# Signs turned and first-step weight sums moved to accumulating DMAs in the Strassen FFNs of a hybrid decoder step

## The chip, the core and the metric

The kernel runs on one core of a Trainium2 chip, in one launch. The metric is the device time of that launch in microseconds, the median of the runs shown. The engines are TensorE (PE, with its weight loads PEld), VectorE (DVE), ScalarE (ACT), GpSimd (POOL) and SyncE (SP, which issues nearly all DMAs).

## The reference

Two layers over 512 prompt rows and 32 sample rows, all fp32. Layer 0 has a gated MLP token mixer, layer 1 forgetting attention; both have two SwiGLU FFNs around the mixer and a gated per-layer embedding behind it:

```python
def swiglu(x, w1, w3, w2):
    return (jax.nn.silu(x @ w1) * (x @ w3)) @ w2
...
        for i in range(DEPTH):
            h = h + 0.5 * swiglu(rmsnorm(h, ffn1_norm[i]), ffn1_w1[i], ffn1_w3[i], ffn1_w2[i])
            xn = rmsnorm(h, mix_norm[i])
...
            h = h + mix
            h = h + 0.5 * swiglu(rmsnorm(h, ffn2_norm[i]), ffn2_w1[i], ffn2_w3[i], ffn2_w2[i])
            gate = jax.nn.sigmoid(rmsnorm(h, ple_norm[i]) @ ple_w_gate[i])
            h = h + gate * (pe[i] @ ple_w_proj[i])
```

D_MODEL is 1024, D_FF 2816, DEPTH 2: four FFNs in all. The change is in these four alone.

## The kernel before

Activations are kept transposed, 128 features by 544 rows (512 prompt, 32 sample), in eight tiles `h`. Every fp32 product is made of three float32r matmuls: an operand is split into a high part (a ScalarE copy with rounding) and the rest (a VectorE subtraction), and hi·hi, hi·lo, lo·hi are added in PSUM. For a weight block the split is `_split` (L190 the ScalarE cast, L191 the VectorE subtraction); `mm` (L233 to L239) does the matmuls.

All weights run through one stream of *pieces*, in the order in which TensorE uses them. `prepare` keeps the stream ahead of the piece in use: inside an FFN splits are made 2 pieces ahead, sums 3 and loads 6 (`self.ahead`). `_load` brings 512 KB by a DMA from SP into one of 44 buffers named `big`.

An FFN begins with four plain pieces (the first 256 columns of w1 and w3, of 48 matmuls each), whose results `gate` in `ffn` (L418 to L421) takes out of PSUM. Meanwhile `forms` (L299 to L306) makes the sums of halves of the activations. Then come ten Strassen steps, each on a 2x2 block of weights `a11, a12, a21, a22` (`seven`), with seven products in the order of `SEVEN = "1562734"` (`products`, L476, 24 matmuls each). Products 1, 2 and 4 use a block as it was loaded, the other four use sums of blocks, made on VectorE by `_sum` (L176), 128x1024 each:

```python
        for k, x, op, y in (("5", a21, "+", a22), ("6", (r, "5"), "-", a11), ("7", a11, "-", a21),
                            ("3", a12, "-", (r, "6"))):
            d[k] = dict(key=(r, k), sum=(x, op, y))
```

Products add into three PSUM tiles: A takes 1, 6, 7, 4, C takes 5, 3, B takes 2. After products 1, 5 and 6 ScalarE copies the tile out (`evict`, L484, to `r1`, `r5`, `r6`) before the next product goes on adding; so product 7, which adds to A, waits for the copy `r6`. From step 2 on, products of the second matrix (w2) stand between these.

Inside the steps (`ffn_steps`) the instruction order of PE, ACT, DVE and POOL is the written one; elsewhere the scheduler sets it. Every engine takes its instructions in order. POOL adds squares of the activations (L318) at an FFN's end, and has little else; no DMA is issued from it. The four FFNs are called FFN 1 to 4 in order of time.

Of the kernel before, what the change touches and what calls it, by code (L numbers as in the profile page):

```python
# [23 lines left out]
F32R = mybir.dt.float32r  # L24
I32 = mybir.dt.int32
AF = mybir.ActivationFunctionType
ALU = mybir.AluOpType
AX = mybir.AxisListType

P = 128  # L30
# [7 lines left out]
HT = T // 2  # L38
# [48 lines left out]
class Builder:  # L87
# [45 lines left out]
    def flat(self, n, dt=F32):  # L133
        return self.big(dt)[:].rearrange("p a b -> p (a b)")[:, :n]

    def add_plain(self, ap):
        r = len(self.aps)
        self.aps.append(ap)
        self.pieces.append(dict(key=(r, 0), src=(r, 0), n=ap.shape[1], sum=None))

    def seven(self, aps):

        r = len(self.aps)
        self.aps.extend(aps[k] for k in (0, 2, 3, 1))
        a11, a21, a22, a12 = ((r + k, 0) for k in range(4))
        d = {k: dict(key=(r, k), src=x, sum=None) for k, x in (("1", a11), ("2", a12), ("4", a22))}
        for k, x, op, y in (("5", a21, "+", a22), ("6", (r, "5"), "-", a11), ("7", a11, "-", a21),
                            ("3", a12, "-", (r, "6"))):
            d[k] = dict(key=(r, k), sum=(x, op, y))
        for v in d.values():  # L150
            v.update(n=1024)
        return d

    def _load(self):
        ap = self.aps[self.a_load]
        raw = self.flat(1024)
        self.nc.sync.dma_start(out=raw[:, :ap.shape[1]], in_=ap)
        self.raws[self.a_load] = raw
        self.a_load += 1

    def _raw(self, x, n):
        r, c = x
        while self.a_load <= r:
            self._load()
        return self.raws[r][:, c:c + n]

    def _sum(self):
        p = self.pieces[self.p_sum]
        self.p_sum += 1
        if p["sum"] is None:  # L170
            return
        a, op, b = p["sum"]
        get = lambda x: self._raw(x, 1024) if isinstance(x[1], int) else self.sums[x]
        a, b = get(a), get(b)
        t = self.flat(1024)
        self.nc.vector.tensor_tensor(t, a, b, ALU.add if op == "+" else ALU.subtract)  # L176
        self.sums[p["key"]] = t

    def _split(self):
        while self.p_sum <= self.p_split:  # L180
            self._sum()
        p = self.pieces[self.p_split]
        n = p["n"]
        src = self.sums[p["key"]] if p["sum"] else self._raw(p["src"], n)
        if n <= 512:
            w = self.flat(1024, F32R)
            hi, lo = w[:, :n], w[:, 512:512 + n]
        else:
            hi, lo = (self.flat(n, F32R) for _ in range(2))
        self.nc.scalar.copy(hi, src)  # L190
        self.nc.vector.tensor_tensor(lo, src, hi.bitcast(F32), ALU.subtract)  # L191
        self.split[self.p_split] = (hi, lo)
        self.p_split += 1

    def prepare(self):

        u, end = self.p_next, len(self.pieces) - 1
        split, sums, load = self.ahead
        while self.p_split <= min(u + split, end):
            self._split()  # L200
        while self.p_sum <= min(u + sums, end):
            self._sum()
        p = self.pieces[min(u + load, end)]
        need = [x for x in (p["sum"][::2] if p["sum"] else [p["src"]]) if isinstance(x[1], int)]
        while self.a_load <= max([r for r, _ in need], default=0):
            self._load()

# [86 lines left out]
    def forms(self, h, gcol, n, xs):  # L294

        nc = self.nc
        x = self.big()
        for a in range(2):
            nc.scalar.activation(x[:, a, :], h[2 * n + a], AF.Copy, scale=self.gain(gcol + 2 * n + a))  # L299
        t13, t24 = self.tmp(), self.tmp()  # L300
        two = lambda t: t.rearrange("p (a b) -> p a b", a=2)
        f13, f24 = self.big(F32R), self.big(F32R)
        nc.vector.tensor_tensor(two(t13), x[:, :, HT:], two(x[:, 0, :]), ALU.subtract)
        self.split_pair(f13, t13)
        nc.vector.tensor_tensor(t24[:, :HT], x[:, 1, HT:], t13[:, :HT], ALU.subtract)
        nc.vector.tensor_tensor(t24[:, HT:], x[:, 1, :HT], t24[:, :HT], ALU.subtract)  # L306
        self.split_pair(f24, t24)
        half = lambda t, b: tuple(x[:, b * HT:(b + 1) * HT] for x in t)
        f13, f24 = ((t[:, 0, :], t[:, 1, :]) for t in (f13, f24))
        return {"1": half(xs[2 * n], 0), "2": half(xs[2 * n + 1], 0), "3": half(xs[2 * n + 1], 1),  # L310
                "5": half(f13, 0), "7": half(f13, 1), "6": half(f24, 0), "4": half(f24, 1)}
    def ssq(self, acc, h, cols=slice(0, T), first=False):

        nc = self.nc
        sq = acc[:, cols] if first else self.tmp()[:, cols]
        nc.scalar.activation(sq, h[:, cols], AF.Square)  # L316
        if not first:
            nc.gpsimd.tensor_tensor(acc[:, cols], acc[:, cols], sq, ALU.add)  # L318
# [60 lines left out]
    def ffn_pieces(self, n):  # L379
        i, d = self.i, {}  # L380
        for f in range(2):
            for w in range(2):
                self.add_plain(i["w13p"][n, w, f])
        for kind, at, k, part in self.ffn_slots():
            if kind == "g":
                if at not in d:
                    d[at] = self.seven([i["w13"][n, at - 1, x] for x in range(4)])
                self.pieces.append(d[at][k])
            elif at < len(PARTS) - 1:
                if k % 2 == 0:  # L390
                    self.aps.append(i["w2a"][n, at, k // 2])
                    d["w"] = len(self.aps) - 1
                src = d["w"], k % 2 * 512
                self.pieces.append(dict(key=src, src=src, n=512, sum=None))
            elif part is None or part[0] == 0:
                self.add_plain(i["w2b"][n, k])
# [36 lines left out]
    def ffn_steps(self, h, xf, rstd, first, on_chunk):  # L433
        nc = self.nc
        add = ALU.add
        tt = nc.vector.tensor_tensor
# [4 lines left out]

        def gate(j, a, g):

            def one():
                tt(g, g, rstd.unsqueeze(1).broadcast_to([P, 2, T]), ALU.mult)  # L445

            def two():
                nc.scalar.activation(g[:, 0], g[:, 0], AF.Silu)  # L448

            def three():  # L450
                tt(g[:, 1], g[:, 1], g[:, 0], ALU.mult)

            def four():
                pair = self.big(F32R)
                self.split_pair(pair, g[:, 1])
                hid[j, a] = pair[:, 0, :], pair[:, 1, :]
            return [one, two, three, four]
# [22 lines left out]
        def evict(j, k):  # L480
            t = tiles[j]
            if k in "156":
                t["r" + k] = q2(self.tmp())
                nc.scalar.copy(t["r" + k], t["C" if k == "5" else "A"])  # L484
                return
            if k == "2":
                t["g"] = self.big(), self.big()
            g = t["g"]
            if k == "2":
                for w in range(2):  # L490
                    tt(g[0][:, w, :HT], t["B"][w], t["r1"][:, w], add)
            elif k == "7":
                tt(g[1][:, :, HT:], t["A"], t["r5"], add)
            elif k == "3":
                tt(g[0][:, :, HT:], t["C"], t["r6"], add)
                todo[0].extend(gate(j, 0, g[0]))
            else:
                nc.scalar.copy(g[1][:, :, :HT], t["A"])  # L498
                todo[1].extend(gate(j, 1, g[1]))
                del tiles[j]  # L500
# [858 lines left out]

# [22 lines left out]
```

## Time and profile before

| | |
|---|---|
| median of 3 runs | 2092.16 us (2091.04 to 2095.01) |
| profiled execution | 2090.37 us, of which the span is 2088.2 |
| PE busy | 2053.9 us, 98% of the span |
| DVE busy | 1521.5 us, 73% |
| ACT busy | 934.8 us, 45% |
| POOL busy | 181.0 us, 9% |
| DMA moved | 237.94 MB, mean 114 GB/s |

In the profile a line L176 is line 176 of the kernel. "issue" is time in which an engine waited for nothing that the profile shows. Starts are counted from the beginning of the span. Matmuls overlap, so the time shown of a group exceeds the distance between the starts of two groups.

### The profile page before, as it was taken

Reading aid. Unit: us, or ns where it says so; the run is one execution under the profiler, and the core shown is the slowest. Engines: PE = TensorE matmul, PEld = TensorE weight load, DVE = VectorE, ACT = ScalarE, POOL = GpSimd, SP = SyncE. Lnnn points to the kernel's source line nnn. Section 1 sums busy time; section 2 is a strip of 40 time slices with the busy share of each in tenths; the row PEclk is TensorE's granted clock in tenths of the full one; section 3 lists DMA queues with packets and bytes.
Section 4 is the critical chain, followed back from the end, with each engine's and each line's share of the span. In section 5 each row is a group of like instructions: output and inputs, shape, how many; then the busy total and the mean of one; then the engine's idle time right before and its main releaser. Section 6 shows DMA issues by size and latency. Waiting matters only on the chain.

```text
span 2088.2 us, 38796 instructions
## 1 busy us (share of the span) xinstructions
PE 2053.9 (98%) x16364; PEld 2016.3 (97%) x16364; DVE 1521.5 (73%) x1893; ACT 934.8 (45%) x1376; POOL 181.0 (9%) x226
## 2 busy tenths in 40 slices
PE   6999999999999999999999999999999999999999
PEld 6999999999999999999999999999977999999999
DVE  7877787556787777776698777786465887777773
ACT  6444344423445344454355344444364654343451
POOL 0000000410100000042050000001041300000020
PEclk9999999999999999999999999999999999999999
DMA  4232324312223232432193322326467322322331
GB/s 163 90 112 73 111 93 140 104 54 71 73 101 117 75 103 81 152 97 81 47 323 148 112 101 91 112 74 198 156 196 267 105 102 72 111 85 98 123 102 44
DMA packets 93776, 237.94 MB, mean 114 GB/s; under 512 B 9490, under 2 KB 27442, under 8 KB 93602
## 3 DMA queue, kind: packets, MB, share of 16 engines
q1 hardware_dynamic: 93458, 235.42, 33.8%
q8 instruction: 129, 2.11, 0.4%
q14 instruction: 45, 0.37, 0.1%
q10 hardware_dynamic: 144, 0.04, 0.0%
HBM read 218.94 MB, written 16.49 MB: 113 GB/s over the span
## 4 chain that ended last, share of the span: by engine, by line
PE 88%; DVE 5%; ACT 3%; DMA 2%; issue 1%; SPq 0%; POOL 0%; ACTq 0%; DVEq 0%; POOLq 0%
PE ps L476 33%; PE ps L233 14%; PE ps L239 14%; PE ps L237 14%; PE pb L476 5%; ACT big L190 1%; DVE big L191 1%; DVE big L176 1%; PE ps L1144 1%; PE ps L1146 1%; PE ps L1145 1%; PE ps L992 0%; PE ps L990 0%; PE ps L1105 0%; DMA big<-in_w13p 0%
## 5 line engine op out<-in xcount | busy, mean ns | idle before, releaser
L476 PE MATMUL ps<-big,big 128*128 128x272 f32 x5760 | 750.2, 289 | 10.6 <-DVE tmp L418 5.3
L476 PEld LDWEIGHTS ps<-big,big 128*128 128x128 f32 x5760 | 735.7, 189 | 12.4 <-ACT tmp L484 6.9
L191 DVE TENSOR_TENSOR big<-big,big 128x1024 fp32r<-128x1024 f32 (+2 forms) x541 | 594.6, 1101 | 107.9 <-ACT big L190 107.7
L190 ACT CAST big<-big 128x1024 fp32r<-128x1024 f32 (+2 forms) x541 | 489.4, 932 | 282.5 <-DVE big L176 275.3
L233 PE MATMUL ps<-big,big 128*128 128x256 f32 x2768 | 576.2, 289 | 12.0 <-ACT big L289 8.8
L239 PE MATMUL ps<-big,big 128*128 128x256 f32 x2768 | 570.9, 288 | 1.0 <-DVE big L191 1.0
L237 PE MATMUL ps<-big,big 128*128 128x256 f32 x2768 | 571.2, 287 | 0.1
L233 PEld LDWEIGHTS ps<-big,big 128*128 128x128 f32 x2768 | 443.5, 189 | 15.4 <-ACT big L289 8.8
L237 PEld LDWEIGHTS ps<-big,big 128*128 128x128 f32 x2768 | 445.9, 189 | 0.6 <-DVE big L290 0.6
L239 PEld LDWEIGHTS ps<-big,big 128*128 128x128 f32 x2768 | 442.8, 188 | 1.8 <-DVE big L191 1.2
L318 POOL TENSOR_TENSOR st<-st,tmp 128x544 f32<-128x544 f32 (+1 forms) x63 | 87.3, 1386 | 1610.9 <-ACT tmp L316 1610.6
L176 DVE TENSOR_TENSOR big<-big,big 128x1024 f32<-128x1024 f32 x160 | 194.9, 1218 | 0.0
L515 DVE SCALAR_TENSOR_TENSOR big<-ps,big 128x544 f32<-128x544 f32 x160 | 115.6, 722 | 106.9 <-PE ps L239 106.7
L484 ACT COPY tmp<-ps 128x544 f32<-128x544 f32 x120 | 73.5, 612 | 146.5 <-PE ps L476 146.2
L476 PE MATMUL pb<-big,big 128*128 128x272 f32 x960 | 127.1, 288 | 0.0
L448 ACT ACTIVATE big<-big 128x544 f32<-128x544 f32 x80 | 52.8, 661 | 161.8 <-DVE big L445 160.0
L476 PEld LDWEIGHTS pb<-big,big 128*128 128x128 f32 x960 | 123.2, 188 | 0.0
L445 DVE TENSOR_TENSOR big<-big,st 128x1088 f32<-128x1088 f32 x80 | 103.2, 1290 | 10.0 <-ACT big L498 8.5
L289 ACT ACTIVATE big<-big,gains 128x544 fp32r<-128x544 f32 (+1 forms) x80 | 55.9, 703 | 118.9 <-DVE big L515 64.9
L278 DVE TENSOR_TENSOR big<-big,big 128x544 fp32r<-128x544 f32 (+1 forms) x96 | 69.5, 724 | 29.0 <-ACT big L277 28.6
L290 DVE SCALAR_TENSOR_TENSOR big<-big,gains,big 128x544 fp32r<-128x544 f32 (+1 forms) x80 | 64.6, 810 | 21.8 <-ACT big L289 21.8
L277 ACT CAST big<-big 128x544 fp32r<-128x544 f32 (+1 forms) x96 | 61.9, 644 | 27.0 <-DVE big L769 15.2
(189 smaller groups left out, 1267.0 us busy)
## 6 DMA issues: line engine op xcount, KB each, us to landing
big<-in_w SPq DMA_DIRECT2D x160, 512.0 KB
big<-in_w2a SPq DMA_DIRECT2D x64, 512.0 KB
big<-in_w2b SPq DMA_DIRECT2D x32, 384.0 KB
big<-in_w13p SPq DMA_DIRECT2D x16, 512.0 KB
big<-in_win SPq DMA_DIRECT2D x16, 512.0 KB
big<-in_wg SPq DMA_DIRECT2D x16, 512.0 KB
big<-in_wkv SPq DMA_DIRECT2D x16, 512.0 KB
big<-in_ck SPq DMA_DIRECT2D x16, 512.0 KB
```

What stands on the lines that cost most here:

```text
L176: self.nc.vector.tensor_tensor(t, a, b, ALU.add if op == "+" else ALU.subtract)
L190: self.nc.scalar.copy(hi, src)
L191: self.nc.vector.tensor_tensor(lo, src, hi.bitcast(F32), ALU.subtract)
L233: i = nc.tensor.matmul(out[:, a:b], wh, xh[:, a:b], start=s, stop=False)
L237: nc.tensor.matmul(out[:, a:b], wh, xl[:, a:b], start=False, stop=False)
L239: nc.tensor.matmul(out[:, a:b], wl, xh[:, a:b], start=False, stop=e)
L278: self.nc.vector.tensor_tensor(pair[:, 1, cols], src, pair[:, 0, cols].bitcast(F32), ALU.subtract)
L318: nc.gpsimd.tensor_tensor(acc[:, cols], acc[:, cols], sq, ALU.add)
L445: tt(g, g, rstd.unsqueeze(1).broadcast_to([P, 2, T]), ALU.mult)
L476: nc.tensor.matmul(dst[w], a[:, c], b, start=k in "152" and kp == 0 and n == 0, stop=kp == NKP - 1 and n == 2, skip_group_check=True)
L484: nc.scalar.copy(t["r" + k], t["C" if k == "5" else "A"])
L515: nc.vector.scalar_tensor_tensor(h[c], whole(out), 0.5, h[c], ALU.mult, ALU.add)
```

## The change

In step 1 of each FFN the four sums are no longer made on VectorE. A block is loaded by SP as before, and further blocks are added onto the same buffer by DMAs that POOL issues with `accum_op=ALU.add` (`_more`). The five buffers are: `u` = a11, later + a21 for product 7; `t` = a21 + a22 for product 5; `v` = a21 + a22 + a11 for product 6, later + a12 for product 3; a12; and a22. "Later" means: issued behind the split that reads the buffer's first content (in `_split`), and so waiting for it. That is five accumulating DMAs of 512 KB per FFN, and 5 SP loads where there were 4. Steps 2 to 10 keep their sums on VectorE. Since a DMA can only add, the signs of all forms are turned: weight sums become additions in all steps, the activation forms are other differences, and one of the two gate results has the opposite sign, which `gate` sets right by a scale of Silu and a scalar factor. The parameter `dynamic_dma_scratch_size` goes from 1024 to 4096.

```diff
-    def seven(self, aps):
-
-        r = len(self.aps)
-        self.aps.extend(aps[k] for k in (0, 2, 3, 1))
-        a11, a21, a22, a12 = ((r + k, 0) for k in range(4))
-        d = {k: dict(key=(r, k), src=x, sum=None) for k, x in (("1", a11), ("2", a12), ("4", a22))}
-        for k, x, op, y in (("5", a21, "+", a22), ("6", (r, "5"), "-", a11), ("7", a11, "-", a21),
-                            ("3", a12, "-", (r, "6"))):
-            d[k] = dict(key=(r, k), sum=(x, op, y))
+    def seven(self, aps, dma):
+
+        a11, a12, a21, a22 = aps
+        if dma:
+            u, t, v = self.add_load(a11), self.add_load(a21, a22), self.add_load(a21, a22, a11)
+            b, d = self.add_load(a12), self.add_load(a22)
+            return {k: dict(key=(t, k), src=(r, 0), n=1024, sum=None, more=more) for k, r, more in (
+                ("1", u, a21), ("5", t, None), ("6", v, a12), ("2", b, None), ("7", u, None), ("3", v, None),
+                ("4", d, None))}
+        r = [self.add_load(x) for x in (a11, a21, a22, a12)]
+        x11, x21, x22, x12 = ((k, 0) for k in r)
+        d = {k: dict(key=(r[0], k), src=x, sum=None) for k, x in (("1", x11), ("2", x12), ("4", x22))}
+        for k, x, y in (("5", x21, x22), ("6", (r[0], "5"), x11), ("7", x11, x21), ("3", x12, (r[0], "6"))):
+            d[k] = dict(key=(r[0], k), sum=(x, y))
...
-        self.nc.sync.dma_start(out=raw[:, :ap.shape[1]], in_=ap)
+        self.nc.sync.dma_start(out=raw[:, :aps[0].shape[1]], in_=aps[0])
+        for ap in aps[1:]:
+            self._more(raw, ap)
...
+    def _more(self, raw, ap):
+        self.nc.gpsimd.dma_start(out=raw, in_=ap, accum_op=ALU.add)
...
-        self.nc.vector.tensor_tensor(t, a, b, ALU.add if op == "+" else ALU.subtract)
+        self.nc.vector.tensor_tensor(t, a, b, ALU.add)
...
         self.nc.vector.tensor_tensor(lo, src, hi.bitcast(F32), ALU.subtract)
+        if p.get("more") is not None:
+            self._more(src, p["more"])
...
-        nc.vector.tensor_tensor(t24[:, :HT], x[:, 1, HT:], t13[:, :HT], ALU.subtract)
-        nc.vector.tensor_tensor(t24[:, HT:], x[:, 1, :HT], t24[:, :HT], ALU.subtract)
...
+        minus = lambda out, a, b: nc.vector.scalar_tensor_tensor(out, a, -1.0, b, ALU.mult, ALU.subtract)
+        minus(t64[:, :HT], t57[:, :HT], x[:, 1, HT:])
+        minus(t64[:, HT:], t64[:, :HT], x[:, 1, :HT])
...
-                    d[at] = self.seven([i["w13"][n, at - 1, x] for x in range(4)])
+                    d[at] = self.seven([i["w13"][n, at - 1, x] for x in range(4)], at == 1)
...
-                nc.scalar.activation(g[:, 0], g[:, 0], AF.Silu)
+                nc.scalar.activation(g[:, 0], g[:, 0], AF.Silu, scale=sign)
...
-                tt(g[:, 1], g[:, 1], g[:, 0], ALU.mult)
+                nc.vector.scalar_tensor_tensor(g[:, 1], g[:, 1], sign, g[:, 0], ALU.mult, ALU.mult)
...
-    nc = _bacc.Bacc("TRN2", target_bir_lowering=False, num_devices=1, dynamic_dma_scratch_size=1024)
+    nc = _bacc.Bacc("TRN2", target_bir_lowering=False, num_devices=1, dynamic_dma_scratch_size=4096)
```

The order of instructions changes at three places that matter below. First VectorE at the start of FFN 1, from the split of product 5's weights to that of product 3's. Before (L191 splits, L176 sums, L303 to L306 and L278 the activation forms, L418 to L421 the gate of the plain pieces):

```order
L191 TENSOR_TENSOR big70_411<-big61_341,big69_410 128x1024
L176 TENSOR_TENSOR big71_414<-big61_341,big32_172 128x1024
L303 TENSOR_TENSOR tmp74_470<-big73_467 128x544
L305 TENSOR_TENSOR tmp75_471<-big73_467,tmp74_470 128x272
L418 TENSOR_TENSOR tmp78_481<-ps63_347,st38_227 128x544
L420 TENSOR_TENSOR tmp79_482<-ps72_418,st38_227 128x544
...
L191 TENSOR_TENSOR big83_518<-big71_414,big82_517 128x1024
L191 TENSOR_TENSOR big85_522<-big49_259,big84_521 128x1024
L176 TENSOR_TENSOR big86_525<-big32_172,big47_255 128x1024
L191 TENSOR_TENSOR big91_557<-big86_525,big90_556 128x1024
L176 TENSOR_TENSOR big92_560<-big49_259,big71_414 128x1024
L191 TENSOR_TENSOR big97_593<-big92_560,big96_592 128x1024
```

And of the change (L203 splits, L318 and L320 forms, L434 and L436 gate; `big33` is t, `big34` v, `big32` u):

```order
L203 TENSOR_TENSOR big69_413<-big33_174,big68_412 128x1024
L318 TENSOR_TENSOR tmp72_470<-big71_467 128x544
L320 SCALAR_TENSOR_TENSOR tmp73_471<-tmp72_470,big71_467 128x272
L434 TENSOR_TENSOR tmp76_481<-ps62_349,st40_234 128x544
L436 TENSOR_TENSOR tmp77_482<-ps70_418,st40_234 128x544
...
L203 TENSOR_TENSOR big81_518<-big34_177,big80_517 128x1024
L203 TENSOR_TENSOR big83_523<-big49_262,big82_522 128x1024
L203 TENSOR_TENSOR big89_558<-big32_172,big88_557 128x1024
L203 TENSOR_TENSOR big94_592<-big34_177,big93_591 128x1024
```

The sums are gone, one more of them ahead of what is shown; the rest keeps its order here. In FFN 2 the forms moreover go ahead of L436, behind which they stood.

Second ScalarE in the same stretch, in the change (L202 casts, L501 the copies r1, r5, r6; a wait on DMASW is one for an accumulating DMA):

```order
L202 CAST big80_517<-big34_177 128x1024 [waits DMASW2_49]
L202 CAST big82_522<-big49_262 128x1024 [waits DMAHW2_49]
L501 COPY tmp87_555<-ps79_492 128x544 [waits PE_49,Activation_49]
L202 CAST big88_557<-big32_172 128x1024 [waits DMASW3_49]
L501 COPY tmp92_589<-ps86_530 128x544 [waits PE_49,Activation_49]
L202 CAST big93_591<-big34_177 128x1024 [waits DMASW4_49]
L501 COPY tmp97_621<-ps79_492 128x544 [waits PE_49,Activation_49]
```

The order is that of before. The cast for product 3 (of `big34`) stands ahead of the copy r6 (to `tmp97`) and now waits for an accumulating DMA where it waited for a VectorE sum.

Third POOL ahead of FFN 3, in the change (`big1492` is t, `big1491` u, `big1493` v; L788 and L335 were there before, next to each other):

```order
L788 COPY ks_112<-big1366_11387 128x32 [waits DVE_49] x2
L173 DMA big1492_12238<-in_w13 128x1024 [waits DMAHW7_49,PE_49]
L173 DMA big1491_12236<-in_w13 128x1024 [waits DMAHW6_49,DVE_49]
L173 DMA big1493_12241<-in_w13 128x1024 [waits DMAHW0_49,DMASW4_49,PE_49]
L173 DMA big1493_12241<-in_w13 128x1024 [waits DMASW4_49]
L173 DMA big1493_12241<-in_w13 128x1024 [waits DMASW5_49,DVE_49]
L335 TENSOR_TENSOR st1946_15998<-st1946_15998,tmp1948_16018 128x544 [waits DMAHW3_49,DMAHW2_49,Activation_49]
```

All five DMA rows are new: one addition to t, one to u, three to v. In FFN 3 the addition to u, which waits for VectorE's split of product 1, stands ahead of all three to v; in FFN 1, 2 and 4 the first two to v stand ahead of it.

## Rows read from the trace of the kernel before

**Rows 1.** The page's first part: busy time, share of the span and instructions of the engines.
```profile
PE 2053.9 (98%) x16364; PEld 2016.3 (97%) x16364; DVE 1521.5 (73%) x1893; ACT 934.8 (45%) x1376; POOL 181.0 (9%) x226
```

**Rows 2.** Busy time by stretch: length, PE, PEld, DVE, ACT, POOL (instructions), granted PE clock, DMA share, GB/s. The body of FFN 1, the start of FFN 2, and two stretches behind gaps of PE (FFN 1, FFN 4).
```profile
64.00:360.00 296.00, 296.00 (x2367) 296.00 (x2366) 230.31 (x264) 128.44 (x177) 0.00 (x0) 1.00 0.31 104
573.80:587.00 13.20, 12.55 (x98) 12.11 (x96) 10.67 (x14) 7.77 (x11) 0.00 (x0) 1.00 0.46 159
46.20:51.20 5.00, 4.99 (x24) 4.81 (x24) 4.70 (x8) 4.11 (x6) 0.00 (x0) 0.60 0.30 122
1685.00:1688.00 3.00, 2.92 (x13) 2.92 (x14) 2.11 (x2) 0.89 (x2) 0.00 (x0) 0.52 0.28 115
```

**Rows 3.** Timeline of PE, L476, at the starts of the four FFNs: start, us, operation, count, idle before and its releaser. 24 matmuls are one product; step 1 begins with products 1, 5, 6, then 2 (on pb), then 7.
```profile
37.77 3.18 PE L476 MATMUL ps<-big,big 128*128 128x272 f32 x24
46.21 5.02 PE L476 MATMUL ps<-big,big 128*128 128x272 f32 x24 [5.26 <-DVE tmp L418]
58.65 18.31 PE L476 MATMUL ps<-big,big 128*128 128x272 f32 x144 [0.88 <-ACT tmp L484]
...
573.85 9.62 PE L476 MATMUL ps<-big,big 128*128 128x272 f32 x72
587.34 4.92 PE L476 MATMUL ps<-big,big 128*128 128x272 f32 x37 [0.84 <-ACT tmp L484]
...
1115.93 6.20 PE L476 MATMUL ps<-big,big 128*128 128x272 f32 x48
1129.71 5.55 PE L476 MATMUL ps<-big,big 128*128 128x272 f32 x42 [0.90 <-ACT tmp L484]
...
1676.80 6.29 PE L476 MATMUL ps<-big,big 128*128 128x272 f32 x48
1685.09 4.82 PE L476 MATMUL ps<-big,big 128*128 128x272 f32 x24 [2.00 <-ACT tmp L484]
1689.74 3.18 PE L476 MATMUL pb<-big,big 128*128 128x272 f32 x24
1692.76 7.44 PE L476 MATMUL ps<-big,big 128*128 128x272 f32 x58
```

**Rows 4.** Timeline of DVE at the start of FFN 1: the first three sums (L176), the gate's first step, and the splits of products 6 and 2 (L191 x2).
```profile
37.18 1.22 DVE L176 TENSOR_TENSOR big<-big,big 128x1024 f32<-128x1024 f32 x1
43.09 1.22 DVE L176 TENSOR_TENSOR big<-big,big 128x1024 f32<-128x1024 f32 x1
45.34 0.72 DVE L418 TENSOR_TENSOR tmp<-ps,st 128x544 f32<-128x544 f32 x1
49.97 2.36 DVE L191 TENSOR_TENSOR big<-big,big 128x1024 fp32r<-128x1024 f32 x2 [0.22 <-ACT big L190]
52.25 1.22 DVE L176 TENSOR_TENSOR big<-big,big 128x1024 f32<-128x1024 f32 x1
```

**Rows 5.** Timeline of ACT at the start of FFN 1: the casts of products 7 and 3 (L190), and the copy r6 (L484) behind the second.
```profile
53.50 1.05 ACT L190 CAST big<-big 128x1024 fp32r<-128x1024 f32 x1 [2.11 <-DVE big L176]
57.03 1.05 ACT L190 CAST big<-big 128x1024 fp32r<-128x1024 f32 x1 [1.97 <-DVE big L176]
57.99 0.60 ACT L484 COPY tmp<-ps 128x544 f32<-128x544 f32 x1
```

**Rows 6.** Timeline of DVE in FFN 2 to 4: in FFN 2 the gate's step that needs the last plain product, two form instructions (L306, L278) right behind it, and the splits of 6 and 2; in FFN 3 the split of product 1, and the splits of 6 and 2; the same two in FFN 4.
```profile
574.72 0.71 DVE L420 TENSOR_TENSOR tmp<-ps,st 128x544 f32<-128x544 f32 x1
575.35 0.43 DVE L306 TENSOR_TENSOR tmp<-big,tmp 128x272 f32<-128x272 f32 x1
575.70 0.71 DVE L278 TENSOR_TENSOR big<-tmp,big 128x544 fp32r<-128x544 f32 x1
...
578.72 2.36 DVE L191 TENSOR_TENSOR big<-big,big 128x1024 fp32r<-128x1024 f32 x2 [0.23 <-ACT big L190]
...
1107.34 1.22 DVE L191 TENSOR_TENSOR big<-big,big 128x1024 fp32r<-128x1024 f32 x1 [0.23 <-ACT big L190]
1121.03 2.36 DVE L191 TENSOR_TENSOR big<-big,big 128x1024 fp32r<-128x1024 f32 x2 [0.23 <-ACT big L190]
...
1683.61 2.36 DVE L191 TENSOR_TENSOR big<-big,big 128x1024 fp32r<-128x1024 f32 x2 [0.22 <-ACT big L190]
```

**Rows 7.** The chain that ended last: two pieces in which it followed a 512 KB load from its issue on SP to the release of its reader (start, us, what).
```profile
15.77 3.54 DMA big<-in_w13p
1062.88 7.01 DMA big<-in_wkv
```

**Rows 8.** Busy time by stretch (columns as in Rows 2), around one 512 KB load that SP issued alone at 561.74.
```profile
562.00:562.50 0.50, 0.50 (x6) 0.50 (x5) 0.46 (x1) 0.00 (x0) 0.00 (x0) 1.00 0.00 0
...
564.50:565.00 0.50, 0.50 (x6) 0.50 (x5) 0.17 (x1) 0.29 (x1) 0.00 (x0) 1.00 0.17 66
```

**Rows 9.** Groups by line of DVE: count, busy us, mean ns; the weight sums, the gate's product, and a SCALAR_TENSOR_TENSOR of the same shape elsewhere.
```profile
L176 DVE TENSOR_TENSOR big<-big,big 128x1024 f32<-128x1024 f32 x160 | 194.9, 1218 | 0.0
L451 DVE TENSOR_TENSOR big<-big 128x544 f32<-128x544 f32 x80 | 57.4, 717 | 0.0
L808 DVE SCALAR_TENSOR_TENSOR big<-big,tmp 128x544 f32<-128x544 f32 x6 | 4.3, 722 | 0.1
```

**Rows 10.** Timelines of SP and POOL: one issue of a 512 KB load, and one of POOL's additions of squares.
```profile
561.74 0.33 SPq L157 DMA_DIRECT2D big<-in_w  x1
551.74 1.37 POOL L318 TENSOR_TENSOR st<-st,tmp 128x544 f32<-128x544 f32 x1 [4.46 <-ACT tmp L316]
```

More of the change, by code (lines that the diff above doesn't have):

```diff
@@ L134, in flat, with add_load @@
         return self.big(dt)[:].rearrange("p a b -> p (a b)")[:, :n]
+    def add_load(self, *aps):
+        self.aps.append(aps)
+        return len(self.aps) - 1
     def add_plain(self, ap):
-        r = len(self.aps)
-        self.aps.append(ap)
+        r = self.add_load(ap)
         self.pieces.append(dict(key=(r, 0), src=(r, 0), n=ap.shape[1], sum=None))
-    def seven(self, aps):
-        r = len(self.aps)
-        self.aps.extend(aps[k] for k in (0, 2, 3, 1))
-        a11, a21, a22, a12 = ((r + k, 0) for k in range(4))
-        d = {k: dict(key=(r, k), src=x, sum=None) for k, x in (("1", a11), ("2", a12), ("4", a22))}
-        for k, x, op, y in (("5", a21, "+", a22), ("6", (r, "5"), "-", a11), ("7", a11, "-", a21),
-                            ("3", a12, "-", (r, "6"))):
-            d[k] = dict(key=(r, k), sum=(x, op, y))
+    def seven(self, aps, dma):
[11 more added lines that the diff above has]
+            d[k] = dict(key=(r[0], k), sum=(x, y))
         for v in d.values():
@@ L154, in _load @@
     def _load(self):
-        ap = self.aps[self.a_load]
+        aps = self.aps[self.a_load]
         raw = self.flat(1024)
-        self.nc.sync.dma_start(out=raw[:, :ap.shape[1]], in_=ap)
+        self.nc.sync.dma_start(out=raw[:, :aps[0].shape[1]], in_=aps[0])
+        for ap in aps[1:]:
+            self._more(raw, ap)
         self.raws[self.a_load] = raw
         self.a_load += 1
+    def _more(self, raw, ap):
+        self.nc.gpsimd.dma_start(out=raw, in_=ap, accum_op=ALU.add)
     def _raw(self, x, n):
@@ L171, in _sum @@
             return
-        a, op, b = p["sum"]
-        get = lambda x: self._raw(x, 1024) if isinstance(x[1], int) else self.sums[x]
-        a, b = get(a), get(b)
+        a, b = (self._raw(x, 1024) if isinstance(x[1], int) else self.sums[x] for x in p["sum"])
         t = self.flat(1024)
-        self.nc.vector.tensor_tensor(t, a, b, ALU.add if op == "+" else ALU.subtract)
+        self.nc.vector.tensor_tensor(t, a, b, ALU.add)
         self.sums[p["key"]] = t
@@ L203, in prepare @@
         p = self.pieces[min(u + load, end)]
-        need = [x for x in (p["sum"][::2] if p["sum"] else [p["src"]]) if isinstance(x[1], int)]
+        need = [x for x in (p["sum"] or [p["src"]]) if isinstance(x[1], int)]
         while self.a_load <= max([r for r, _ in need], default=0):
@@ L299, in forms @@
             nc.scalar.activation(x[:, a, :], h[2 * n + a], AF.Copy, scale=self.gain(gcol + 2 * n + a))
-        t13, t24 = self.tmp(), self.tmp()
+        t57, t64 = self.tmp(), self.tmp()
         two = lambda t: t.rearrange("p (a b) -> p a b", a=2)
-        f13, f24 = self.big(F32R), self.big(F32R)
-        nc.vector.tensor_tensor(two(t13), x[:, :, HT:], two(x[:, 0, :]), ALU.subtract)
-        self.split_pair(f13, t13)
-        nc.vector.tensor_tensor(t24[:, :HT], x[:, 1, HT:], t13[:, :HT], ALU.subtract)
-        nc.vector.tensor_tensor(t24[:, HT:], x[:, 1, :HT], t24[:, :HT], ALU.subtract)
-        self.split_pair(f24, t24)
+        f57, f64 = self.big(F32R), self.big(F32R)
+        q = x[:].rearrange("p a (c b) -> p (a c) b", c=2)
+        nc.vector.tensor_tensor(two(t57), q[:, 0::3, :], q[:, 1:2, :].broadcast_to([P, 2, HT]), ALU.subtract)
+        self.split_pair(f57, t57)
+        minus = lambda out, a, b: nc.vector.scalar_tensor_tensor(out, a, -1.0, b, ALU.mult, ALU.subtract)
+        minus(t64[:, :HT], t57[:, :HT], x[:, 1, HT:])
+        minus(t64[:, HT:], t64[:, :HT], x[:, 1, :HT])
+        self.split_pair(f64, t64)
         half = lambda t, b: tuple(x[:, b * HT:(b + 1) * HT] for x in t)
-        f13, f24 = ((t[:, 0, :], t[:, 1, :]) for t in (f13, f24))
+        f57, f64 = ((t[:, 0, :], t[:, 1, :]) for t in (f57, f64))
         return {"1": half(xs[2 * n], 0), "2": half(xs[2 * n + 1], 0), "3": half(xs[2 * n + 1], 1),
-                "5": half(f13, 0), "7": half(f13, 1), "6": half(f24, 0), "4": half(f24, 1)}
+                "5": half(f57, 0), "7": half(f57, 1), "6": half(f64, 0), "4": half(f64, 1)}
     def ssq(self, acc, h, cols=slice(0, T), first=False):
@@ L390, in ffn_pieces @@
                 if k % 2 == 0:
-                    self.aps.append(i["w2a"][n, at, k // 2])
-                    d["w"] = len(self.aps) - 1
+                    d["w"] = self.add_load(i["w2a"][n, at, k // 2])
                 src = d["w"], k % 2 * 512
@@ L442, in gate @@
         def gate(j, a, g):
+            sign = 1.0 - 2 * a
             def one():
```

## The prediction

> **What bounds the kernel now.** The page's first part comes first [rows 1]: TensorE is busy 98% of the span, VectorE 73%. That alone says that work taken off VectorE is worth nothing unless it stands where TensorE waits. So the next view is busy time by stretch [rows 2]: in the body of FFN 1 (64 to 360 us) TensorE is busy all 296 us at full clock. There is nothing to gain there; the sums of steps 2 to 10 are covered. What is left is the start of each FFN, and the timeline of TensorE [rows 3] shows it. One product takes 3.02 us (1689.74 to 1692.76). Product 7 is the fifth in order, so without a wait it starts 4 x 3.02 = 12.08 us behind product 1. It starts late by:
>
> - FFN 1: 58.65 - (37.77 + 12.08) = 8.80 us
> - FFN 2: 587.34 - 585.93 = 1.41
> - FFN 3: 1129.71 - 1128.01 = 1.70
> - FFN 4: 1692.76 - 1688.88 = 3.88
>
> That is 15.8 us, 0.76% of the time, and all that this change can reach. Part of it is clock: behind gaps of 5.26 and 2.00 us the granted clock is 0.60 and 0.52 (near 1.2 GHz instead of 2.4), and the next product takes 5.02 and 4.82 us, 1.8 to 2.0 too many; behind gaps of 0.84 us it stays 1.00 [rows 2, 3].
>
> VectorE's timeline in FFN 1 [rows 4] shows why TensorE waits there: two sums (37.18, 43.09) lie ahead of the gate's step at 45.34 that frees the PSUM tile for product 5, and of the splits of products 6 and 2 at 49.97; two more follow [rows 4, 5]. ScalarE's timeline [rows 5] shows the last link: product 7 waits for the copy r6, and r6 stands behind the cast for product 3, which waits for the fourth sum. From the start of that cast to product 7 it is 58.65 - 57.03 = 1.62 us. The gap before 7 is about 0.9 us in three FFNs with a releaser "ACT tmp L484" [rows 3], which is this copy.
>
> **The change, part by part.**
>
> *Removed:* 16 sums of 1.22 us each [rows 9], four per FFN. Started back to back they take about 1.15. Two lie ahead of the split of product 6, so this split can end 2.3 us earlier where VectorE sets the pace:
>
> - FFN 1: it ended at 49.97 + 1.22 = 51.2 [rows 4], now 48.9. Product 5 can start 2.3 earlier too, at 43.9, still behind a gap of 3.0 us [rows 3], so I keep 4.8 us for it: 48.7. Product 6 starts with its split, 48.9, product 2 follows, and 7 could start 6.04 us later, at 55.0.
> - FFN 4: 1684.8 [rows 6], now 1682.5. Product 6 no longer waits; 7 could start at 1688.9.
> - FFN 2: here the gate's second step (574.72 [rows 6]) needs the last plain product, which ends when product 1 starts, 573.85. So it can move by 0.7 only; but two form instructions that ran behind it, of 0.43 and 0.71 us [rows 6] and some 0.1 less back to back, stand ahead of it after the change. The split of 6, which ended at 579.9, ends at 578.2.
>
> *Added, the price that decides:* product 3's weights are now ready when an accumulating DMA has landed that can start only when VectorE has split product 6. Call a the time from the end of that split to the start of the cast for product 3: POOL's wake-up and issue, the transfer, its completion. Product 7 starts 1.62 us behind that cast. The trace has no accumulating DMA and none from POOL. Lower bound: a plain 512 KB load, 3.54 us from issue to its reader [rows 7]; an addition moves no less. Upper bound: the longest such piece, 7.01 us, among stores and other loads [rows 7]. I take 5.6: the plain 3.54, plus one more pass of the 2.1 us (562.5 to 564.6) in which a lone load keeps the DMA engines at work [rows 8], since an addition must also read what it adds to. Two prices hidden in a stay open: POOL's issue, between SP's 0.33 us and one POOL instruction of 1.37 [rows 10]; I take 1.0 where issues queue.
>
> By the Trainium skill, "DMA: Bandwidth & Descriptors", section "Anatomy of one DMA — SWDGE (gpsimd) path", a DMA from GpSimd takes about 2.0 us plus its bytes at 436 GB/s. By it a would be an estimate of 3.2 us, and every FFN but the first would run at TensorE's pace.
>
> *FFN 1, 2, 4:* product 7 starts at split + a + 1.62, or at TensorE's bound. FFN 1: 48.9 + 5.6 + 1.6 = 56.1, gain 2.5. FFN 2: 585.4, bound 585.9, gain 1.4. FFN 4: 1689.7, gain 3.0. The other additions there have room: t, u and v's first two are issued early, and their casts come 10 us or more later.
>
> *FFN 3, the place where it costs:* POOL takes its instructions in order, and here the addition to u, which waits for VectorE's split of product 1 (ends 1107.34 + 1.22 = 1108.6 [rows 6]), stands ahead of all three additions to v. So v's first starts at 1109.6 (POOL's issue, 1.0), lands 5.6 later plus 1.0 for sharing the engines with u: 1116.2. The second must wait for it: 1121.8. Then cast (1.05) and split (1.22) of product 6: 1124.1, where it was 1122.25. Then the third, and 1.62: 1124.1 + 5.6 + 1.6 = 1131.3. Loss 1.6.
>
> The same page and section says that DMA engines do not wait on semaphores: the wait happens on the issuing sequencer. By that rule the queue stands still as I assume; were it not so, FFN 3 would gain 1.7 instead, and the sum would be 8.6. The trace of before has no DMA from POOL to show it.
>
> *Edits with one answer:* the gate's product becomes SCALAR_TENSOR_TENSOR, 717 against 722 ns [rows 9]; the two narrow form instructions change alike, 16 times each, on the same engine, so under 0.2 us in all. Additions for subtractions, and a scale in Silu, are the same instructions. The six extra transfers per FFN meet a DMA share of 0.3 to 0.46 [rows 2]; if that cover went, loads for step 2 would come late, which is inside the upper bound of a. POOL is idle 91% of the span; its additions of squares stand ahead of the new rows in FFN 1 to 3, and in FFN 4 one or two stand behind rows that wait only for loads.
>
> *Sum:* 2.5 + 1.4 - 1.6 + 3.0 = 5.3 us. The profiled execution took 2090.37; with the change 2085.1. The median of the runs is 1.8 higher, so **2086.9**.
>
> **The rivals.**
>
> 1. *The addition lands early* (a up to 4.5). Gains reach their caps, 3.65 + 1.4 + 1.7 + 3.9 = 10.6: 2081.5. For it: 3.54 measured for a plain load. Against it: two reads instead of one.
> 2. *The addition lands late* (a = 7). FFN 1: 1.1. FFN 2: 0.5. FFN 3 pays three times: 15.2 - 3a = -5.8. FFN 4: 1.6. In FFN 1, 3 and 4 the gap before 7 passes 2 us, so 1.8 us of slow clock each. Sum: -2.6 - 5.4 = -8.0: 2100.2. It decides from a = 6.7 on, where the loss passes 0.2%. For it: the casts for 7 and 3 stall ScalarE, behind which r5 and r6 queue, and a load among others took 7.01. Against it: DMA is half idle at these places.
> 3. *The wait only changes its name* (a about 6.3): gains of FFN 1, 2 and 4 (5.4) are eaten by FFN 3 (-3.7) and one slow product (-1.8): 2092.2. For it: a is uncertain by more than the margin.
>
> **How the numbers follow.** With a the sum is 8.1 - a (at most 3.65), 7.5 - a (1.4), 15.2 - 3a (1.7), 8.6 - a (3.9). A measurement can tell about 0.2%, 4.2 us, from no change; the sum passes +4.2 at a = 5.85 and -4.2 at a = 6.7. My chances: forecast 0.38 (a from 4.5 to 6, own range 2082 to 2089), rival 1 0.15, rival 3 0.22, rival 2 0.25. Part of the forecast (a above 5.85) counts as same. Faster 0.50, same 0.24, slower 0.26. The range reaches from rival 1's caps to the bound of 7.01: 2081 to 2100.
>
> **What would show it.** Right: the L476 product 7 of FFN 1 starts near 56 and of FFN 4 13 us behind product 1; DVE is busy 16 x 1.22 = 19.5 us less; FFN 3 shows ScalarE waiting for a DMA ahead of the cast of product 6. Each step is read from the waits of L202: "DMA" as releaser, and its length gives a. Wrong: a below 4.5 or above 6.7, FFN 3 without that wait, or a new gap of TensorE outside the four starts.

## Result and profile after

The changed kernel takes 2099.95 us in the median of 6 runs (2098.49 to 2103.13), against 2092.31 (2090.64 to 2095.17) of the kernel before in the same comparison. The ratio is 1.0036, 95% interval 1.0026 to 1.0046: by the ratio it is 7.5 us slower (5.4 to 9.6). I had forecast 2086.9, so the direction is wrong; the range (2081 to 2100) just holds the value.

The page of the profiled execution (2098.85 us, span 2096.8), first part:

```profile
PE 2055.3 (98%) x16364; PEld 2017.9 (96%) x16364; DVE 1503.3 (72%) x1877; ACT 934.7 (45%) x1376; POOL 197.7 (9%) x246
```

VectorE has 18.2 us less work, near the 19.5 forecast, and yet the time rose: the answer is in the four starts. TensorE's timeline there, L493 (columns as in [rows 3], which it answers; 24 matmuls are one product):

```profile
38.04 3.17 PE L493 MATMUL ps<-big,big 128*128 128x272 f32 x24
44.39 8.95 PE L493 MATMUL ps<-big,big 128*128 128x272 f32 x48 [3.17 <-DVE tmp L434]
...
61.16 15.09 PE L493 MATMUL ps<-big,big 128*128 128x272 f32 x108 [4.80 <-ACT tmp L501]
...
577.54 9.23 PE L493 MATMUL ps<-big,big 128*128 128x272 f32 x72
...
590.25 9.93 PE L493 MATMUL ps<-big,big 128*128 128x272 f32 x77 [0.45 <-ACT tmp L501]
...
1118.56 6.20 PE L493 MATMUL ps<-big,big 128*128 128x272 f32 x48
1132.74 4.64 PE L493 MATMUL ps<-big,big 128*128 128x272 f32 x24 [7.97 <-ACT tmp L501]
1137.21 3.19 PE L493 MATMUL pb<-big,big 128*128 128x272 f32 x24
1140.58 9.69 PE L493 MATMUL ps<-big,big 128*128 128x272 f32 x75 [0.17 <-ACT tmp L501]
...
1687.38 9.64 PE L493 MATMUL ps<-big,big 128*128 128x272 f32 x72
...
1701.17 11.06 PE L493 MATMUL ps<-big,big 128*128 128x272 f32 x86 [1.12 <-ACT tmp L501]
```

How late product 7 is, its start less that of product 1 less 12.08, is the measure for all that follows (us):

| | FFN 1 | FFN 2 | FFN 3 | FFN 4 | sum |
|---|---|---|---|---|---|
| before [rows 3] | 8.80 | 1.41 | 1.70 | 3.88 | 15.8 |
| after | 11.04 | 0.63 | 9.94 | 1.71 | 23.3 |

The sum grew by 7.5 us. FFN 2 and 4 gained, FFN 1 and above all FFN 3 lost. FFN 1 costs 1.2 us more than the table shows: from its product 7 to FFN 2's product 1 it is 516.4 us where it was 515.2, because behind the gap of 4.80 us the granted clock is 0.50 (1.2 GHz) from 61 to 64. The two together are 8.7 us; the spans of the two traces differ by 8.6.

The chain of waits names what came between, in pieces from POOL's issue of an addition to the start of its reader (start, us):

```profile
49.68 9.85 DMA big<-in_w
582.41 6.20 DMA big<-in_w
...
1112.03 12.26 DMA big<-in_w
1124.57 5.53 DMA big<-in_w
1132.83 6.05 DMA big<-in_w
1693.78 5.70 DMA big<-in_w
```

Four of the six are 5.5 to 6.2 us. The two long ones are FFN 1's addition of a12 (9.85) and FFN 3's first addition to v (12.26); both lie beyond the upper bound of 7.01 that the prediction set. Busy time by stretch (columns as in [rows 2]) shows what stood beside them. First one stretch of plain loads and the addition of 1124.57, which has the DMA engines to itself (a DMA share of 1 means that all 16 are busy; GB/s times us is KB):

```profile
24.00:25.00 1.00, 1.00 (x11) 1.00 (x10) 0.95 (x2) 0.98 (x2) 0.00 (x0) 1.00 1.02 418
...
1126.00:1127.00 1.00, 0.00 (x0) 0.00 (x0) 0.00 (x0) 0.00 (x0) 0.00 (x0) 1.00 1.01 90
1127.00:1128.00 1.00, 0.00 (x0) 0.00 (x0) 0.00 (x0) 0.00 (x0) 0.00 (x0) 1.00 0.89 164
1128.00:1129.00 1.00, 0.00 (x0) 0.00 (x0) 0.00 (x0) 0.00 (x0) 0.00 (x0) 1.00 1.05 209
1129.00:1130.00 1.00, 0.00 (x0) 0.00 (x0) 0.00 (x0) 0.00 (x0) 0.00 (x0) 0.51 0.33 62
```

The shares add up to 3.28 us, the bytes to 525 KB: one addition of 512 KB fills all DMA engines for 3.3 us, where a plain load at 418 GB/s takes 1.25. So 5.5 us is 3.3 on the engines and 2.2 around them. This is one addition against loads in their densest stretch. By the same sum over shares the lone load of [rows 8] took 1.5 us (shares of 0.60, 0.45, 0.96, 0.84 and 0.17 in the half microseconds from 562.5). The page of the change has all of them, by queue (packets, MB, share of the 16 engines over the span; q1 has the DMAs of SP, q0 the 20 additions):

```profile
q1 hardware_dynamic: 94034, 237.52, 33.6%
q0 software_dynamic: 2880, 10.49, 2.8%
```

That is 2.9 us for a mean addition, and 1.6 us for 512 KB of the rest. So an addition is worth about 3 us of all engines, two to two and a half loads.

Then the two places of the long additions, before and after:

```profile
48.00:60.00 12.00, 10.90 (x76) 10.47 (x76) 9.18 (x10) 7.58 (x10) 0.00 (x0) 0.91 0.27 88
1109.00:1124.00 15.00, 14.63 (x117) 14.40 (x117) 14.23 (x20) 8.55 (x12) 0.00 (x0) 1.00 0.25 88
```

```profile
48.00:60.00 12.00, 8.36 (x58) 8.14 (x57) 3.59 (x3) 3.48 (x6) 0.86 (x1) 0.90 0.94 303
1109.00:1124.00 15.00, 15.00 (x123) 15.00 (x122) 10.71 (x16) 8.26 (x12) 2.67 (x3) 1.00 1.04 298
```

DMA engines that were three quarters idle are full. In FFN 3 three additions stand there in a row, t, u and v (two in the second line), then v's second; POOL had waited 14.38 us for t's load, and so they all go out late, the first 8.8 us ahead of product 1:

```profile
1109.77 0.92 POOL L173 DMA_DIRECT2D big<-in_w  x1 [14.38 <-DMA big<-in_w]
1111.49 1.75 POOL L173 DMA_DIRECT2D big<-in_w  x2 [0.81 <-DVE big L203]
1124.57 0.86 POOL L173 DMA_DIRECT2D big<-in_w  x1 [11.33 <-DMA big<-in_w]
```

At 3.3 us each the three are 9.9 of the 15.6 us that the engines were busy from 1109 to 1124; the rest are loads from SP. In FFN 1 it is a burst of six loads from SP (47.74 and 50.54) around the addition; SP's timeline before, then after:

```profile
42.37 8.96 SPq L157 DMA_DIRECT2D big<-in_w  x4
54.77 10.52 SPq L157 DMA_DIRECT2D big<-in_w2a  x2
```

```profile
47.74 2.37 SPq L166 DMA_DIRECT2D big<-in_w  x5
50.54 18.55 SPq L166 DMA_DIRECT2D big<-in_w2a  x2
```

### The profile page after: what moved, and what is told of

It reads as the page before. It is cut to its first block, busy times and chain, and to the rows that moved or that the text cites. A ratio compares the mean times of both kernels' runs of the same rounds, so it can differ in the third digit from the quotient of the medians.

```text
span 2096.8 us, 38852 instructions
## 1 busy us (share of the span) xinstructions
PE 2055.3 (98%) x16364; PEld 2017.9 (96%) x16364; DVE 1503.3 (72%) x1877; ACT 934.7 (45%) x1376; POOL 197.7 (9%) x246
## 4 chain that ended last, share of the span: by engine, by line
PE 89%; DMA 4%; DVE 3%; ACT 2%; issue 1%; POOL 1%; SPq 0%; ACTq 0%; POOLq 0%; DVEq 0%
PE ps L493 33%; PE ps L247 15%; PE ps L253 14%; PE ps L251 14%; PE pb L493 5%; DMA big<-in_w 3%; DVE big L203 1%; PE ps L1161 1%; PE ps L1163 1%; PE ps L1162 1%; ACT big L202 1%; PE ps L1009 0%; PE ps L1007 0%; PE ps L1122 0%; DVE big L292 0%
## 5 line engine op out<-in xcount | busy, mean ns | idle before, releaser
L493 PE MATMUL ps<-big,big 128*128 128x272 f32 x5760 | 751.7, 289 | 17.8 <-ACT tmp L501 14.5
L493 PEld LDWEIGHTS ps<-big,big 128*128 128x128 f32 x5760 | 737.6, 190 | 19.3 <-ACT tmp L501 16.0
L203 DVE TENSOR_TENSOR big<-big,big 128x1024 fp32r<-128x1024 f32 (+2 forms) x541 | 594.4, 1101 | 132.3 <-ACT big L202 130.3
L202 ACT CAST big<-big 128x1024 fp32r<-128x1024 f32 (+2 forms) x541 | 489.3, 931 | 295.4 <-DVE big L188 258.7
L247 PEld LDWEIGHTS ps<-big,big 128*128 128x128 f32 x2768 | 443.1, 189 | 15.6 <-ACT big L303 8.9
L335 POOL TENSOR_TENSOR st<-st,tmp 128x544 f32<-128x544 f32 (+1 forms) x63 | 87.7, 1392 | 1512.1 <-ACT tmp L333 1511.7
L188 DVE TENSOR_TENSOR big<-big,big 128x1024 f32<-128x1024 f32 x144 | 175.3, 1218 | 0.0
L501 ACT COPY tmp<-ps 128x544 f32<-128x544 f32 x120 | 73.8, 615 | 146.6 <-PE ps L493 146.3
L493 PE MATMUL pb<-big,big 128*128 128x272 f32 x960 | 127.1, 288 | 0.0
L493 PEld LDWEIGHTS pb<-big,big 128*128 128x128 f32 x960 | 123.3, 188 | 0.0
L303 ACT ACTIVATE big<-big,gains 128x544 fp32r<-128x544 f32 (+1 forms) x80 | 55.9, 704 | 119.1 <-DVE big L532 64.9
```

The source lines that it names most:

```text
L188: self.nc.vector.tensor_tensor(t, a, b, ALU.add)
L247: i = nc.tensor.matmul(out[:, a:b], wh, xh[:, a:b], start=s, stop=False)
L493: nc.tensor.matmul(dst[w], a[:, c], b, start=k in "152" and kp == 0 and n == 0, stop=kp == NKP - 1 and n == 2, skip_group_check=True)
```

## Experiments

Theory D: an addition is work of 3.3 us on all DMA engines, and the loss is where that work meets other transfers. Rivals: W, the wait behind the split as such; Q, u's place ahead of v on POOL in FFN 3; S, the turned signs or the scratch. All ratios are to the kernel before, with the 95% interval.

**1. All sums on VectorE** (one argument of `seven`: `at == 1` becomes `False`).

> All sums back on VectorE; the turned signs, the SCALAR_TENSOR_TENSOR forms and the larger scratch stay. Theory D (the loss of the change lies where an accumulating DMA meets busy DMA engines: in FFN 1, where its addition of a12 took 9.9 us, and in FFN 3, where the first addition to v took 12.3 us): 2092.3 +- 1.5, the starts of the four FFNs as before (late by 8.8, 1.4, 1.7, 3.9). Rival W (the wait for the split, then for the addition, is the whole cost): the same. Rival S (the turned signs or the scratch cost something): 2096 to 2100.

2093.95 us, ratio 1.0005 (0.9996 to 1.0014), no difference that can be told. Lateness 8.77, 1.41, 1.67, 3.85: that of before. S falls: the signs, forms and scratch cost nothing that can be told at these places. D and W forecast the same here. That a DMA can only add, as the section on the change has it, is not shown: every addition of these runs is an `ALU.add`, and no other was tried.

**2. Not in FFN 3** (`at == 1 and n != 2`).

> Accumulating DMAs in FFN 1, 2 and 4, VectorE sums in FFN 3. By the traces FFN 3 lost 8.2 us from the start of product 1 to that of product 7, so theory D says 2099.95 - 8.2 = 2091.7 +- 1.5, with FFN 1 still 2.2 (3.4 with the slow clock) behind before and FFN 4 2.2 ahead. Rival: the loss of FFN 3 is not local (loads pushed later all along): over 2095.

2093.36 us, 1.0007 (0.9999 to 1.0016). FFN 3 is late by 1.68 again, the others by 11.40, 0.23 and 2.14. FFN 3's loss is local. The remaining three together are no gain: FFN 1 eats what FFN 2 and 4 win.

**3. Four loads less in FFN 1 and in FFN 3.**

```diff
...
-        r = [self.add_load(x) for x in (a11, a21, a22, a12)]
+        r = again or [self.add_load(x) for x in (a11, a21, a22, a12)]
...
```

> As the change, but in FFN 1 and 3 step 2 has no loads of its own: it uses step 1's blocks a12 and a22 again, so four SP loads of 512 KB fall away in each (the output is another). Theory D: in FFN 1 the addition of a12 meets two loads instead of six, takes about 6.5 us from issue instead of 9.9, and product 7 starts 3.4 to 4.8 us earlier (1.5 more if the slow clock goes); in FFN 3 the first addition to v takes 8 to 9 us instead of 12.3. Sum 2091 to 2094. Rivals W (the wait itself) and Q (the order on POOL's queue, u ahead of v in FFN 3): both additions take what they took, 2099 to 2100.

2094.95 us, 1.0010 (1.0001 to 1.0019), 1 us above what D allowed. The chain of waits shows the two additions, and v's second behind the first:

```profile
49.89 6.42 DMA big<-in_w
...
1109.14 10.09 DMA big<-in_w
1119.51 6.78 DMA big<-in_w
```

FFN 1 went as D says: 6.42 us instead of 9.85, late by 7.42 instead of 11.04, with wait and order untouched, so W falls there. FFN 3 is a half miss: 10.09, where I had said 8 to 9, and product 7 was hardly earlier (late by 9.65), since v's second addition took 6.78 us instead of 5.53. Here u went out right behind t, without waiting for a split, and v's addition right behind u: Q's hold was gone and the loss was not. What was left were three additions in a row.

**4. Product 3's weights on VectorE.**

```diff
...
-                ("1", u, a21), ("5", t, None), ("6", v, a12), ("2", b, None), ("7", u, None), ("3", v, None),
-                ("4", d, None))}
+                ("1", u, a21), ("5", t, None), ("6", v, None), ("2", b, None), ("7", u, None), ("4", d, None))
+                } | {"3": dict(key=(t, "3"), n=1024, sum=((b, 0), (v, 0)))}
```

> As the change, but the weights of product 3 are a VectorE sum again (a12 + v), so no addition waits for the split of product 6. Theories D and W: in FFN 1, 2 and 4 product 7 starts 12.1 us behind product 1 or behind the gap of product 5 (FFN 1: at 56.4 instead of 61.2, with 1.5 less of slow clock; FFN 2: 0.6 earlier; FFN 4: 1.7 earlier); FFN 3 keeps its 8 us ahead of product 6. Sum 2099.95 - 6.3 - 0.6 - 0.2 - 1.7 = 2091.2. If the addition of a12 costs by its traffic and not by being waited for: about the same time again, 2090 to 2092. If the sums of VectorE are what it hides: 2097 or more.

2092.39 us, 0.9999 (0.9991 to 1.0008), as forecast within 1.2. Late by 7.00, 0, 10.72 and 0.38. D and W forecast the same here too; what falls is that the sums of VectorE were what the addition hid. With no addition on the path the early ones pay in three FFNs, and FFN 3 keeps its gap ahead of product 6:

```profile
1127.57 5.22 PE L493 MATMUL ps<-big,big 128*128 128x272 f32 x24 [7.95 <-ACT tmp L501]
```

**5. Half an addition** (`_split` adds only 512 of a12's 1024 columns).

> As the change, but the late addition of a12 covers half the columns, 256 KB (the output is another). Theory D (the time on the DMA engines, 3.3 us for 512 KB, is the part of an addition that counts, the rest of about 2.3 us is fixed): from POOL's issue to its reader 6.2 and 5.7 us in FFN 2 and 4 become 4.5 and 4.1, in FFN 1 9.9 becomes about 8, and product 7 starts 1.7 us earlier in FFN 1, 3 and 4, 0.6 in FFN 2: about 2094.5. Rival F (an addition has a fixed price whatever its size): nothing moves, 2099 to 2100.

In FFN 2 the addition and its reader (POOL, then ACT), and FFN 1's in the chain of waits:

```profile
579.31 0.86 POOL L173 DMA_DIRECT2D big<-in_w  x1 [11.02 <-DVE big L203]
583.86 1.05 ACT L202 CAST big<-big 128x1024 fp32r<-128x1024 f32 x1 [2.56 <-DMA big<-in_w]
```

```profile
49.80 7.90 DMA big<-in_w
```

4.55 us in FFN 2 (4.5 expected), 4.22 in FFN 4 (4.1), 7.90 in FFN 1 (8): the price goes with the bytes, and F falls. The time, 2098.05 us (1.0035; 1.0023 to 1.0048), is above the 2094.5 expected. The traced execution took 2093.63, at a mean granted clock of 0.998, the others 2097.46 to 2100.33 at 0.993 to 0.995, so the trace speaks for its own execution alone.

**6. Without u's addition in FFN 3** (`more` of product 1 set to `None` there).

> As the change, but in FFN 3 the addition of a21 to u is left out (product 7 then uses a11 alone; the output is another). Theory D (each addition holds all DMA engines for some 3.3 us, and they run one after another): the first addition to v lands 9 us behind its issue instead of 12.3, and product 7 of FFN 3 starts 3.3 to 4 us earlier: 2096 to 2097. Rival Q (u's place in POOL's order is the whole loss of FFN 3): the first addition to v takes 5.5 to 6, product 7 8 us earlier: 2091.8. Rival W (only the wait for the split of product 6 costs): unchanged, 2099 to 2100.

```profile
1110.57 10.10 DMA big<-in_w
1120.95 6.89 DMA big<-in_w
```

The first addition to v took 10.10 us instead of 12.26, its second 6.89 instead of 5.53, and product 7 is late by 8.41 instead of 9.94. That is D's direction and half its size; Q's 5.5 to 6 is far off. Q may still have a share: without u's wait v's first addition went out 8.2 us ahead of product 1, where it was 6.5 (0.7 of that because t went out earlier). The time settles nothing: 2103.03 us (1.0059; 1.0040 to 1.0079), above what any of the three forecast, from 2096.65 to 2108.1, the two longest at a mean granted clock of 0.991. In the traced execution (2099.03) the 1.5 us that FFN 3 gained were lost again ahead of FFN 4, by the clock (last section).

**7. v alone in FFN 3** (there t is a21, u stays a11, and step 2 has no loads of its own).

> As the change, but in FFN 3 only v gets additions (products 5 and 7 use a21 and a11 alone) and step 2 has no loads of its own (the output is another). Theory D (additions and loads share the DMA engines; an addition that has them to itself takes 5.5 to 6 us from issue to reader): the first addition to v lands 5.5 to 6.5 us behind its issue instead of 12.3, the second as before (5.5), and product 7 of FFN 3 starts 1 to 4 us late instead of 9.9: 2099.95 - 6 to 9 = 2091 to 2094. Rival L (the first addition to v is long for a reason of its own, say because its load has just landed or because it follows an idle stretch of POOL's queue): 10 us or more again, product 7 8 us late or more, 2098 or more.

POOL's timeline, and product 7:

```profile
1112.00 0.91 POOL L174 DMA_DIRECT2D big<-in_w  x1 [16.70 <-DMA big<-in_w]
1117.79 0.86 POOL L174 DMA_DIRECT2D big<-in_w  x1 [4.88 <-DMA big<-in_w]
```

```profile
1132.83 13.36 PE L496 MATMUL ps<-big,big 128*128 128x272 f32 x105 [0.76 <-ACT tmp L504]
```

The first addition to v takes 5.79 us instead of 12.26, with the same place behind its own load; L falls. Its second took 5.45. Product 7 is late by 2.26 instead of 9.94. 2094.70 us, 1.0009 (0.9999 to 1.0020), 5.3 below the change, a little less than D's 6 to 9. Removing four loads gave 2.2 us of v's 12.26, removing u 2.2; with t gone too it is 6.5. No single neighbour is the cause; this run takes away three at once and does not part them.

**8. What follows from it**: FFN 3 on VectorE, and product 3 on VectorE in the others (edits 2 and 4 together).

> FFN 3 wholly on VectorE sums, and in FFN 1, 2 and 4 product 3's weights a VectorE sum; additions by DMA only for products 5, 6 and 7 of those three. Theory D: product 7 late by 7.0, 0, 1.7 and 0.4 as in the runs that had each of these, 9.1 in sum against 15.8 of before: 2092.3 - 6.7 = 2085.6, between 2084 and 2088. Rival S (something outside the four starts costs as much): 2090 to 2093.

2083.33 us, ratio 0.9968 (0.9956 to 0.9981): 6.7 us faster than before by the ratio, as worked out (8.0 by the medians, with 2091.35 before in this comparison; one of the six executions took 2091.22, at a mean granted clock of 0.994). Product 7 in FFN 1 to 4 is late by 7.17, 0, 1.68 and 0 (in FFN 4 counted from product 2 at 1684.45, as records of product 1 are missing there):

```profile
57.41 18.21 PE L493 MATMUL ps<-big,big 128*128 128x272 f32 x144
...
584.52 18.20 PE L493 MATMUL ps<-big,big 128*128 128x272 f32 x144
...
1126.52 18.31 PE L493 MATMUL ps<-big,big 128*128 128x272 f32 x144 [0.93 <-ACT tmp L501]
...
1687.47 18.20 PE L493 MATMUL ps<-big,big 128*128 128x272 f32 x144
```

## Why the prediction was wrong

- **What bounds the kernel** held. The four starts and what follows the first are nearly all that moved: 7.5 us more lateness and 1.2 of clock behind FFN 1's product 7, against 8.6 between the two traces and 7.6 between the medians.
- **The sums removed** did what was said: in FFN 1 product 5 starts at 44.39 (43.9 forecast) and the split of 6 ends at 49.4 (48.9), with the whole kernel 0.3 later by then.
- **The addition alone** was priced nearly right: 5.5 to 6.2 us from issue to reader, 0.3 more from the split, so 5.8 to 6.5 against a = 5.6. With it FFN 2 gained 0.8 (1.4 forecast) and FFN 4 2.2 (3.0). The Trainium skill's 2.0 us plus bytes at 436 GB/s ("DMA: Bandwidth & Descriptors", section "Anatomy of one DMA — SWDGE (gpsimd) path"), an estimate of 3.2 us here, is too low for an addition: the trace shows 2.2 us for the fixed part, near it, but 3.3 us for the transfer. The Trainium skill's rule in the same section, that the wait happens on the issuing sequencer, agrees: POOL stood 11.33 us ahead of v's second addition.
- **The step that failed** is the one on shared DMA engines: "The six extra transfers per FFN meet a DMA share of 0.3 to 0.46", so hidden, and in FFN 3 "1.0 for sharing the engines with u". I costed an addition as a delay and not as work. At 3.3 us each, five additions are 16.4 us of full DMA engines per FFN, and in FFN 3 three of them go out within 2.3 us. The wait that the prediction named there, ahead of the cast of product 6, came, but longer. V's first addition was issued 6.5 us ahead of product 1 (6.3 forecast), but took 12.26 us and not 6.6: that is 5.7 of the 6.6 us that FFN 3 lost beyond the forecast. The upper bound of 7.01 came from a plain load and did not hold for an addition. Experiment 7 gives the forecast's own chain once the neighbours are gone (5.79 and 5.45).
- **FFN 1**: a was 10.2 instead of 5.6, so a gain of 2.5 became a loss of 2.2, and 1.2 more of clock. Experiment 3 brings it back to 6.4 from issue to reader. I had looked at the share in the body and at FFN 2, not here; the trace of before showed 0.27, and what filled it was the change itself and the loads that it delayed.
- **Rival 2** (late landing) named 2100.2 and the right sign, but its a = 7 everywhere is not what happened: a is 5.8 to 6.5 where the engines are free and over 10 where they are not. FFN 4 gained where it said 0.2 lost. That its sum, and with it the end of the range, lies at the measured time is chance.
- **No extra gap** outside the starts, and the edits with one answer cost nothing that experiment 1 can tell.

What stays open: how additions and loads divide the engines among them. Experiments 3, 6 and 7 show that each neighbour adds its part, but not why one addition less gave 2.2 us where 3.3 were expected, nor why v's second addition grew by 1.3 to 1.4 us in experiments 3 and 6.

## What to carry to other kernels

Price a transfer that is put in the place of arithmetic twice: as a delay, and as time on the DMA engines, which for an addition here was two to two and a half times that of a load of the same size. Read the DMA share in the very microseconds where the transfer will run, add to it what the change itself puts there, and keep a late transfer off the path: the same change, with the last sum left on VectorE and without the FFN whose loads come late, is by the ratios 6.7 us faster than before instead of 7.5 slower.

## What the runs showed of the hardware

SP reads a page table by register loads while FFN 1 starts, ahead of the loads of step 2. They slowed down while additions were under way, from 27 us on. From 23 to 26 us plain loads filled the DMA engines as well (shares of 1.01 to 1.05), and the reads from 22 to 27 us took 263 to 275 ns; so full engines alone do not do it. Whether it is the additions on the engines or POOL's work for them is not shown. Their line before, then after (count, duration ns min/median/max, first and last start):

```profile
L914 SPq TENSOR_LOAD <-pt x35: 262/263/283, 20.4 to 41.7; - x35
```

```profile
L931 SPq TENSOR_LOAD <-pt x35: 262/268/1447, 21.7 to 47.1; - x35
```

The loads of step 2 stand behind these reads on SP, and so SP's burst came at 47.74 instead of being spread from 42.37 on. The maximum was 1.1 us or more in experiments 2 to 8, whose FFN 1 has additions, and 273 ns in experiment 1, which has none.

One set of gaps had two outcomes for TensorE's clock. Between FFN 3 and FFN 4 TensorE has three gaps of 0.9, 0.6 and 1.8 us within 6 us, alike in all ten traces. Behind them the granted clock stayed at 1.00 before, in the change and in experiments 2 and 5, and fell to 0.50 (1.2 GHz) for some microseconds in the other six. From product 7 of FFN 3 to product 1 of FFN 4 it is 546.8 to 547.1 us in the first four and 548.0 to 549.0 in the six. Just behind the third gap, before and then in experiment 1 (columns as in [rows 2]):

```profile
1630.00:1631.00 1.00, 1.00 (x10) 1.00 (x10) 1.00 (x1) 0.64 (x1) 1.00 (x2) 1.00 0.00 0
```

```profile
1631.00:1632.00 1.00, 1.00 (x6) 1.00 (x6) 1.00 (x1) 0.58 (x1) 1.00 (x2) 0.50 0.00 0
```

So one to two microseconds of a single execution can be this and not the edit. Only one execution of each kernel was traced; where the clock was low in the others is not known.
